# Attention logits with a 64-row second pass for two heads at once, and four steps put in another order

## Chip, cores and metric

One core of a Trainium2 chip runs the whole program. The metric is the device time of one execution in microseconds (us); less is better. Times of before: 2449.05, 2453.21 and 2453.59 us, median 2453.21.

## What is computed

Two sequences (512 and 256 tokens, width 1024) go through two layers in f32. They are held together as T = 768 tokens in six blocks of 128. A layer is:

```python
xn = rmsnorm(x, norm1_g[l]); z = xn @ w_in[l]
o_a = mixer_a(...)   # gelu, layer norm, a 128x128 mix inside each block
o_b = mixer_b(...)   # 8 query heads, 2 key heads, band of 3 blocks, bias and sink
o_c = mixer_c(...)   # 8 query heads, 2 key heads, all keys, q and k normed and rotated
merged = sum(sigmoid(xn @ w_gate + b_gate) * (o_n @ w_branch_n))
x = x + merged @ w_out[l]
x = x + conv_ffn(rmsnorm(x, norm2_g[l]), ...)   # up, conv of width 3, silu * val, down
```

A head has 64 channels, and its logits are q . k / 8, an inner product over 64.

## The kernel before

**Precision.** The large products are made of float32r passes, where an operand is its rounded part (hi) plus the rest (lo): w_hi x_hi + w_hi x_lo + w_lo x_hi, so three matmuls (L435, L564, L1121) for each product. ScalarE (ACT) writes each hi of a weight (L327, L337), VectorE (DVE) each lo (`Stream.flush`, L357). Weights arrive by DMA through SyncE (SP) into `raw` tiles and quarter tiles `qa` to `qd`; the FFN's up projection works with seven products P1 to P7 in place of eight (`piece`, L1110), for which GpSimd (POOL) adds quarters with accumulating DMAs (`sum1` to `sum4`, L275).

**Logits.** `attention` (L722) has 24 units in each of B and C per layer: a pair of heads (i) times a block of queries (n). `stage_a` (L742) makes the logits of head e of a unit, w = 256, 384 or 512 keys wide. A head's stationary operand has q_hi on 64 rows and q_lo on the other 64; the moving operand `kb[:, 0]` has k_hi on both halves, `kb[:, 1]` has k_lo on both. Two matmuls on 128 rows, one for each, add up to the logits of one head (L757). Then DVE adds the bias and takes the minimum (L766, L771), ACT takes the exponential (L768, L772), `stage_n` divides, `stage_b` transposes the probabilities (L796), and `stage_c` multiplies them with v (L809): there head 0 fills columns 0 to 63 of the array and head 1 columns 64 to 127. An order written out by hand sets the steps of a unit: `ORDER` = a of head 0, b0 of the unit before, n0, a1, c of two units before, b1, n1. Each step is a yield of a generator that the dense products pump between their own matmuls (`pump`, L400), so PE goes from a dense product to one attention step and back.

**Other places that the change touches.**
- `sumsq` (L494) squares one of eight x tiles on ACT and adds it to a sum. Tiles 2 to 5 are added by accumulating DMAs that POOL issues (L508), into two sums (even and odd tiles), the rest on DVE (L504, L506). `rstd_tok` (L510) sums over channels on PE (L514), POOL takes the power -1/2 (L520); `rstd_diag` and `rstd_bc` spread it over the partitions (L530 to L546). In layer 0 `rstd_tok` stands in the middle of the first dense product; in the FFN it stands after piece P5 of the first group, and `rstd_bc` after P1 of the second.
- The rotary tables of C: two tables g, each of two broadcast DMAs of 192 KB in packets of 256 bytes (L885), then DVE multiplies (L888). This is issued ahead of the key and value product of C (`dense_tok`, L958).
- The convolution of the FFN: `later(n, f)` (L422) runs a step after n ticks; a dense product ticks once per k (six matmuls), a piece twice. `CHAIN` gives the ticks of a group's steps (scale, centre tap on ACT, two outer taps on DVE, silu, product, hi, lo), `CHAIN_END` those of the last group, after which few down products are left. Both outer taps were one step, `taps` (L1061).
- `qknorm` (L891) writes q of C as [hi, lo] on the rows for both heads.

Of the kernel before, what the change touches and what calls it, by code (L numbers as in the profile page):

```python
# [18 lines left out]
P = 128  # L19
D = 1024  # L20
KD = D // P
# [9 lines left out]
D_FF = 2816  # L31
NJ = D_FF // P
FFC = [(0, 3), (3, 3), (6, 3), (9, 3), (12, 3), (15, 3), (18, 4)]
CHAIN = (2, 4, 6, 9, 11, 13, 15)
CHAIN_END = (1, 2, 3, 5, 6, 7, 8)
TAIL = 5
HT = T // 2
HW = T + 3
# [91 lines left out]
def encoder_kernel(ctx, tc, x_d, w_d, vec_d, ln_d, rope_d, gqk_d, oneh_d, relb_d, mask_d, id_d, y_d):  # L130
# [61 lines left out]
    def fl(ap):  # L192
        return ap.bitcast(F32)
# [215 lines left out]
    def finish_bg(n=0):  # L409
        while len(bg) > n:  # L410
            if next(bg[0][0], "end") == "end":
                bg.pop(0)
# [78 lines left out]
        if k is not None:  # L491
            sumsq(x_ap, k, new=lambda: unit(F32)[:, 0])

    def sumsq(x_ap, k, dve=False, new=None):  # L494

        n = x_ap.shape[-1]
        c = 0 if dve else k % 2
        sq = (new or page)()[:, 0:n]
        ACT.activation(sq, x_ap, AF.Square)
        if k == c:  # L500
            st["acc", c] = sq
            return
        if dve or k >= KD - 2:
            DVE.tensor_tensor(st["acc", 0], st["acc", 0], sq, ALU.add)  # L504
            if not dve and k == KD - 2:
                DVE.tensor_tensor(st["acc", 0], st["acc", 0], st.pop(("acc", 1)), ALU.add)  # L506
        else:
            POOL.dma_start(out=st["acc", c], in_=sq, accum_op=ALU.add)  # L508
# [69 lines left out]
    def layer_mixers(l, xs):  # L578
# [143 lines left out]
        def attention(qs, kbs, vtok, out, bias):  # L722
# [19 lines left out]
            def stage_a(u, e):  # L742
                i, si, b0, nb, n, lo, hi = units[u]
                w = (hi - lo) * P
                if e == 0:
                    if bias:
                        fetch(i)
                        fetch(i + 1)
                        nbt.pop(i - 1, None)
                    wt = 388 if bias else 512  # L750
                    S[u] = dict(lg=page(T + 8) if bias else [page(512), page(512)], nm=small(2), rs=small(4))
                s = S[u]
                ps = sps()
                kb = kbs[i // 2]
                q = qs[i][:, e, n * P:(n + 1) * P]
                for c in range(2):
                    PE.matmul(out=ps[:, 0:w], lhsT=q, rhs=kb[:, c, lo * P:hi * P], start=c == 0, stop=c == 1)  # L757
                mn = s["nm"][:, e:e + 1]
                su = s["rs"][:, e:e + 1]
                if bias:  # L760
                    lg = s["lg"][:, e * 388:e * 388 + w + 1]
                    h = 2 * i + e
                    j0 = (lo - n + 1) * P
                    sink = st["ns"][:, h:h + 1]
                    POOL.tensor_copy(lg[:, w:w + 1], sink)
                    DVE.tensor_tensor_reduce(lg[:, 0:w], ps[:, 0:w], nbt[i][:, e * 384 + j0:e * 384 + j0 + w],  # L766
                                             1.0, sink, ALU.add, ALU.min, accum_out=mn)
                    ACT.activation(lg, lg, AF.Exp, bias=mn, scale=-1.0, accum_out=su)  # L768
                else:
                    lg = s["lg"][e][:, 0:w]  # L770
                    DVE.tensor_tensor_reduce(lg, ps[:, 0:w], zero.broadcast_to([P, w]), 1.0, BIG, ALU.add, ALU.min, accum_out=mn)  # L771
                    ACT.activation(lg, lg, AF.Exp, bias=mn, scale=-1.0, accum_out=su)  # L772
# [109 lines left out]
        for g in range(2):  # L882
            gt = page()
            for s in range(2):
                POOL.dma_start(  # L885
                    out=gt[:, s * 384:(s + 1) * 384],
                    in_=bass.AP(gqk_d.tensor, gqk_d.offset + ((l * 2 + g) * 2 + s) * HD, [[0, P], [0, NT], [1, HD]]))
            DVE.scalar_tensor_tensor(gt, cs, -(HD ** -0.5) if g == 0 else 1.0, gt, ALU.mult, ALU.mult)  # L888
            tab.append(gt)

        def qknorm(z, nh, tb, cats, dst):  # L891
            n = nh * HD
            t1, t2 = (unit(F32).rearrange("p a b -> p (a b)")[:, 0:NT * n] for _ in range(2))

            def v4(u):
                return u.rearrange("p (t h d) -> p t h d", t=NT, d=HD)

            z4, t14, t24 = v4(z), v4(t1), v4(t2)
            ACT.activation(t2, z, AF.Square)
            yield  # L900
            cg = tb[:, 0:384].rearrange("p (t d) -> p t d", t=NT).unsqueeze(2)
            sg = tb[:, 384:768].rearrange("p (t d) -> p t d", t=NT).unsqueeze(2)
            DVE.tensor_tensor(t14, z4, cg.broadcast_to([P, NT, nh, HD]), ALU.mult)
            ss = small(24)[:, 0:NT * nh]
            DVE.tensor_reduce(ss, t2.rearrange("p (a d) -> p a d", d=HD), AX.X, ALU.add)
            DVE.tensor_scalar(ss, ss, 1.0 / HD, EPS, ALU.mult, ALU.add)
            rr = small(24)[:, 0:NT * nh]
            POOL.tensor_tensor(rr, ss, neghalf[:, 0:NT * nh], ALU.pow)
            yield
            for a in range(2):  # L910
                o, i = slice(a * 32, a * 32 + 32), slice(32 - a * 32, 64 - a * 32)
                DVE.tensor_tensor(t24[:, :, :, o], z4[:, :, :, i],
                                  sg[:, :, :, o].broadcast_to([P, NT, nh, 32]), ALU.mult)
            yield
            DVE.tensor_tensor(t1, t1, t2, ALU.add)
            yield
            t13 = t1.rearrange("p (a d) -> p a d", d=HD)
            DVE.tensor_tensor(t13, t13, rr.unsqueeze(2).broadcast_to([P, NT * nh, HD]), ALU.mult)
            yield
            us = []  # L920
            for i in range(2):
                u = unit()
                u4 = u.rearrange("p a b -> p (a b)").rearrange("p (t e x) -> p t e x", t=NT, e=2)
                if cats == "k":
                    for r in range(2):
                        ACT.activation(u4[:, :, 0, r * HD:(r + 1) * HD], t14[:, :, i], AF.Copy)
                else:
                    ACT.activation(u4[:, :, :, 0:HD], t14[:, :, 2 * i:2 * i + 2], AF.Copy)
                us.append(u4)
                yield  # L930
            for i, u4 in enumerate(us):
                if cats == "k":
                    for r in range(2):
                        DVE.tensor_tensor(u4[:, :, 1, r * HD:(r + 1) * HD], t14[:, :, i], fl(u4[:, :, 0, 0:HD]), ALU.subtract)
                else:
                    DVE.tensor_tensor(u4[:, :, :, HD:2 * HD], t14[:, :, 2 * i:2 * i + 2], fl(u4[:, :, :, 0:HD]), ALU.subtract)
                yield
            yield
            for u4 in us:
                u = unit()  # L940
                for e in range(2):
                    yield from tr6(lambda t: u4[:, t, e, :], identr,
                                   lambda ps, a, b: ACT.activation(u[:, e, a:b], ps, AF.Copy))
                dst.append(u)
# [12 lines left out]

        dense_tok(("in2", l, 1792 + 512, 0), ("in2", l, 1792 + 512, 1), xs, evac_kv)  # L958
        finish_bg()
        start_bg(qknorm(zk, 2, tab[1], "k", kc), BG_N)  # L960
        for c in range(2):
            z = flat(unit(F32))
# [75 lines left out]
    def layer_ffn(l, xs2, x_mid, x_spill):  # L1038
# [19 lines left out]
            ACT.activation(f, h[:, 1:770], AF.Identity, scale=cw(1, ct), bias=vec[:, VCB + ct:VCB + ct + 1])  # L1058
            return f

        def taps(f, h, ct):  # L1061
            DVE.scalar_tensor_tensor(f, h[:, 0:769], cw(0, ct), f, ALU.mult, ALU.add)
            DVE.scalar_tensor_tensor(f, h[:, 2:771], cw(2, ct), f, ALU.mult, ALU.add)

        def scaled(h):
            DVE.tensor_tensor(h[:, 1:770], h[:, 1:770], st["bcg"][:, 1:770], ALU.mult)  # L1066
# [1 line left out]
        def conv_v(g):  # L1068
            s = G[g]
            hv = s["h"][:, 1]  # L1070

            def c():
                s["fv"] = centre(hv, NJ + g)
            for n, f in zip(CHAIN_END if g == NJ - 1 else CHAIN,
                            (lambda: scaled(hv), c, lambda: taps(s["fv"], hv, NJ + g))):
                later(n, f)

        def conv_g(g):
# [23 lines left out]
                hs[g] = u  # L1102
                del G[g]
            for n, f in zip(CHAIN_END if g == NJ - 1 else CHAIN,
                            (lambda: scaled(hg), c, lambda: taps(s["fg"], hg, g), si, mu, hi, lo)):
                later(n, f)

        RIGHT = ((1 + HT, 513, 0, 512 - HT), (514, 770, 512 - HT, HT))
# [55 lines left out]
        def evac(c, m, cuts, ps):  # L1164
            last = c == len(FFC) - 1
            final_ = last and l == DEPTH - 1
            if final_:
                t0, t1 = cuts
                xa = st["xu"][m // 2][:, m % 2, t0:t1]
                DVE.tensor_tensor(xa, ps[:, 0, 0:t1 - t0], xa, ALU.add)  # L1170
                sumsq(xa, m, dve=True)
                if t0 and m == 2:
                    finish_bg()
                if m == KD - 1:
# [16 lines left out]
        for s in steps:  # L1191
            if s[0] == "pc":
                piece(s[1], s[2])
                if (s[1], s[2]) == (0, "P5"):
                    rstd_tok()
                    rstd_diag()
                elif (s[1], s[2]) == (1, "P1"):
# [56 lines left out]
    with tc.manual_schedule():  # L1254
# [17 lines left out]
        for k in range(KD):  # L1272
# [13 lines left out]
                W.split()  # L1286
                W.flush()
            if k > 2:
                sumsq(xu[(k - 3) // 2][:, (k - 3) % 2], k - 3)
        for k in range(KD - 3, KD):  # L1290
            sumsq(xu[k // 2][:, k % 2], k)
        del u, xu
        spill = [dram.tile([P, T], F32, name=f"sp{k}") for k in range(KD)]
        x_mid = [dram.tile([P, T], F32, name=f"xm{k}") for k in range(KD)]
# [135 lines left out]
```

## Time and profile before

| | |
|---|---|
| median of three runs | 2453.21 us |
| the profiled execution, its own time | 2457.03 us |
| its span, first to last instruction | 2455.3 us |
| mean granted TensorE clock | 0.989 of full |
| busy: PE / DVE / ACT / POOL | 97 / 62 / 45 / 11 % |
| moved by DMA | 328 MB |

PE is TensorE's matmul, PEld its weight load. In a row of a timeline the first number is the start, the second the duration of that row; a wait in brackets is the engine's idle time just before it and what ended it. In rows of groups the shape is rows*columns of the array, output <- input, then the count, and after the bar busy us and the mean ns of one. The parts of the kernel by time: start and mixer A to 120 us, mixers B and C to 552, projection out to 704, FFN to 1230; the second layer repeats it.

### The profile page before, as it was taken

The numbers are of one execution on the slowest core, as the hardware profiler recorded it, in microseconds if no ns is written. First come the engines' busy times: TensorE is split into PE (matmuls) and PEld (weight loads), VectorE is DVE, ScalarE is ACT, GpSimd is POOL, SyncE is SP. The second block draws the span as 40 slices with busy tenths as digits, with TensorE's granted clock in tenths as the row PEclk, the third lists the DMA queues.
The fourth block names the chain that finished last, engine by engine and source line by source line (L and its number), as shares of the span: only waits on it lengthen the run. The fifth ranks groups of instructions, "written<-read, shape, count | busy, mean of one in ns | idle before, by whom it ended". The sixth has DMA issues, their size and how long they took to land.

```text
span 2455.3 us, 38491 instructions
## 1 busy us (share of the span) xinstructions
PE 2388.1 (97%) x14990; PEld 2315.9 (94%) x14990; DVE 1523.8 (62%) x2656; ACT 1110.0 (45%) x2184; POOL 260.3 (11%) x390
## 2 busy tenths in 40 slices
PE   7999999999999999999999999999999999999997
PEld 7998999889989999999999999998899899999996
DVE  4555535554558777777645554555445687777785
ACT  4344434662345444444433443456424554444452
POOL 1000110000122111111000000100001211111100
PEclk8999999999999999999999999999999999999998
DMA  5511231012467888887732113210135688888854
GB/s 159 108 52 57 52 64 61 27 35 73 137 161 173 244 225 231 230 228 209 219 108 62 57 50 63 61 45 34 44 102 161 145 221 230 228 230 227 227 160 147
DMA packets 134950, 328.24 MB, mean 134 GB/s; under 512 B 15976, under 2 KB 29416, under 8 KB 134768
## 3 DMA queue, kind: packets, MB, share of 16 engines
q1 hardware_dynamic: 101232, 251.83, 31.6%
q0 software_dynamic: 33536, 73.95, 17.0%
q8 instruction: 118, 1.93, 0.3%
q14 instruction: 64, 0.52, 0.1%
HBM read 243.93 MB, written 52.43 MB: 121 GB/s over the span
## 4 chain that ended last, share of the span: by engine, by line
PE 85%; DMA 5%; DVE 4%; ACT 3%; issue 2%; POOL 0%; SPq 0%; POOLq 0%; DVEq 0%; ACTq 0%
PE d L435 47%; PE ga L1121 12%; PE gb L1121 9%; PE d L564 8%; PE s L809 3%; PE s L796 2%; PE s L757 2%; DMA qc<-w_pk 2%; DMA pg<-gqk 1%; DVE wl L357 1%; PE s L669 1%; ACT wh L327 1%; DMA qd<-qc 1%; DMA raw<-w_pk 1%; DMA pg<-pg 0%
## 5 line engine op out<-in xcount | busy, mean ns | idle before, releaser
L435 PE MATMUL d<-u,wh 128*128 128x384 f32 x4480 | 990.1, 343 | 6.8 <-ACT pg L1086 6.3
L435 PEld LDWEIGHTS d<-u,wh 128*128 128x128 f32 x4480 | 782.6, 189 | 21.8 <-issue 11.0
L435 PE MATMUL d<-u,wl 128*128 128x384 f32 x2240 | 575.3, 338 | 0.0
L435 PEld LDWEIGHTS d<-u,wl 128*128 128x128 f32 x2240 | 408.0, 188 | 0.0
L357 DVE TENSOR_TENSOR wl<-raw,wh 128x512 fp32r<-128x512 f32 (+1 forms) x261 | 248.4, 953 | 232.5 <-ACT wh L337 180.8
L1121 PE MATMUL ga<-u,wh 128*128 128x384 f32 x1408 | 364.5, 340 | 7.6 <-ACT u L1129 4.4
L1121 PE MATMUL gb<-u,wh 128*128 128x384 f32 x1056 | 271.0, 338 | 1.9 <-DVE u L1131 1.9
L1121 PEld LDWEIGHTS ga<-u,wh 128*128 128x128 f32 x1408 | 257.1, 189 | 9.5 <-ACT u L1129 5.0
L564 PE MATMUL d<-wh,u 128*128 128x256 f32 x1344 | 248.3, 285 | 3.0 <-ACT u L596 1.9
L1121 PE MATMUL ga<-u,wl 128*128 128x384 f32 x704 | 238.7, 339 | 0.0
L564 PEld LDWEIGHTS d<-wh,u 128*128 128x128 f32 x1344 | 210.9, 191 | 5.2 <-ACT u L596 3.1
L564 PE MATMUL d<-wl,u 128*128 128x256 f32 x672 | 190.7, 284 | 4.9 <-DVE wl L357 4.8
L1121 PEld LDWEIGHTS gb<-u,wh 128*128 128x128 f32 x1056 | 191.6, 188 | 2.7 <-ACT wh L327 1.8
L337 ACT ACTIVATE wh<-raw 128x1024 fp32r<-128x1024 f32 x129 | 135.3, 1049 | 104.3 <-PE d L564 44.9
L1121 PE MATMUL gb<-u,wl 128*128 128x384 f32 x528 | 178.0, 337 | 0.0
L1058 ACT ACTIVATE pg<-u,vec 128x769 f32<-128x769 f32 x88 | 91.0, 1034 | 124.5 <-DVE u L1066 82.0
L1180 DVE TENSOR_TENSOR pg<-d,pg 128x768 f32<-128x768 f32 x104 | 99.5, 956 | 76.5 <-PE d L435 76.0
L564 PEld LDWEIGHTS d<-wl,u 128*128 128x128 f32 x672 | 128.6, 191 | 5.5 <-DVE wl L357 5.2
L1121 PEld LDWEIGHTS ga<-u,wl 128*128 128x128 f32 x704 | 133.2, 189 | 0.0
L662 DVE TENSOR_TENSOR u<-s,u 128x128 fp32r<-128x128 f32 (+1 forms) x112 | 36.9, 329 | 114.5 <-ACT u L661 114.3
L757 PE MATMUL s<-u,u 128*128 128x256 f32 (+2 forms) x384 | 99.9, 342 | 2.2 <-ACT pg L797 1.6
L768 ACT ACTIVATE pg<-pg,sm 128x257 f32<-128x257 f32 (+1 forms) x96 | 52.5, 547 | 109.1 <-DVE sm L766 104.7
(204 smaller groups left out, 3190.1 us busy)
## 6 DMA issues: line engine op xcount, KB each, us to landing
raw<-w_pk SPq DMA_DIRECT2D x174, 512.0 KB, 3.7
pg<-xm SPq DMA_DIRECT2D x104, 384.0 KB, 4.6
xm<-pg SPq DMA_DIRECT2D x96, 384.0 KB, 3.4
u<-w_pk SPq DMA_DIRECT2D x96, 192.0 KB, 3.6
qa<-w_pk SPq DMA_DIRECT2D x44, 256.0 KB, 3.8
qb<-w_pk SPq DMA_DIRECT2D x44, 256.0 KB, 3.2
qc<-w_pk SPq DMA_DIRECT2D x44, 256.0 KB, 3.2
qd<-w_pk SPq DMA_DIRECT2D x44, 256.0 KB, 3.5
```

The costliest lines, as they stand in the source:

```text
L337: ACT.activation(hi[:, :n], t[:, :n], AF.Copy)
L357: DVE.tensor_tensor(lo, t, fl(hi), ALU.subtract)
L435: PE.matmul(out=ps[:, h, 0:b - a], lhsT=w, rhs=x[:, a:b], start=first and i == 0 and pi == 0, stop=last and i == nk - 1 and pi == 2,)
L564: PE.matmul(out=outs[t], lhsT=x, rhs=w, start=k == 0 and pi == 0 and t % 2 == 0, stop=k == KD - 1 and pi == 2, skip_group_check=True)
L662: DVE.tensor_tensor(u[:, 1, a:b], ps, fl(u[:, 0, a:b]), ALU.subtract)
L757: PE.matmul(out=ps[:, 0:w], lhsT=q, rhs=kb[:, c, lo * P:hi * P], start=c == 0, stop=c == 1)
L768: ACT.activation(lg, lg, AF.Exp, bias=mn, scale=-1.0, accum_out=su)
L796: PE.transpose(ps[:, b * P:(b + 1) * P], lg[:, b * P:(b + 1) * P], ident)
L809: PE.matmul(out=ps[e * HD:(e + 1) * HD, 0:P], lhsT=vtok[:, (lo + b) * P + kv * HD:(lo + b) * P + (kv + 1) * HD], rhs=pT, start=b == 0, sto ...
L1058: ACT.activation(f, h[:, 1:770], AF.Identity, scale=cw(1, ct), bias=vec[:, VCB + ct:VCB + ct + 1])
L1121: PE.matmul(out=o, lhsT=a[:, w], rhs=x[:, b], start=p in ("P1", "P2", "P5") and kp == 0 and pi == 0, stop=kp == 3 and pi == 2, skip_group_ ...
L1180: DVE.tensor_tensor(h2(xa), ps[:, :, 0:384], h2(xa), ALU.add)
```

## The change

Head 1's logits are made in head 0's step. Of each head's two matmuls the second keeps only the rows of q_hi (64), so that head 0's is on rows 0 to 63 and head 1's on rows 64 to 127; the order is (head 0, 128 rows), (head 0, 64), (head 1, 64), (head 1, 128). C's q is laid out for it as B's was: q_hi of head 1 on the upper rows. In the start, the squares are added one after another by DVE and POOL instructions. `rstd_tok` of the FFN comes after P6, one piece sooner. The tables are multiplied after the key and value product. The two outer taps are two steps, with new ticks.

```diff
-CHAIN = (2, 4, 6, 9, 11, 13, 15)
-CHAIN_END = (1, 2, 3, 5, 6, 7, 8)
+CHAIN = (2, 4, 6, 7, 9, 11, 13, 15)
+CHAIN_END = (1, 2, 4, 5, 6, 8, 9, 10)
...
-    def sumsq(x_ap, k, dve=False, new=None):
+    def sumsq(x_ap, k, eng=None, new=None):
-        c = 0 if dve else k % 2
+        c = 0 if eng else k % 2
...
-        if dve or k >= KD - 2:
-            DVE.tensor_tensor(st["acc", 0], st["acc", 0], sq, ALU.add)
-            if not dve and k == KD - 2:
+        if eng or k >= KD - 2:
+            (eng or DVE).tensor_tensor(st["acc", 0], st["acc", 0], sq, ALU.add)
+            if not eng and k == KD - 2:
...
-                ps = sps()
-                kb = kbs[i // 2]
-                q = qs[i][:, e, n * P:(n + 1) * P]
-                for c in range(2):
-                    PE.matmul(out=ps[:, 0:w], lhsT=q, rhs=kb[:, c, lo * P:hi * P], start=c == 0, stop=c == 1)
+                if e == 0:
+                    kb = kbs[i // 2]
+                    s["ps"] = [sps(), sps()]
+                    for a, c in ((0, 0), (0, 1), (1, 1), (1, 0)):
+                        r = slice(a * HD, a * HD + HD) if c else slice(0, P)
+                        PE.matmul(out=s["ps"][a][:, 0:w], lhsT=qs[i][r, a, n * P:(n + 1) * P], rhs=kb[r, c, lo * P:hi * P],
+                                  start=a == c, stop=a != c)
+                ps = s["ps"][e]
...
-            DVE.scalar_tensor_tensor(gt, cs, -(HD ** -0.5) if g == 0 else 1.0, gt, ALU.mult, ALU.mult)
             tab.append(gt)
...
-                    ACT.activation(u4[:, :, :, 0:HD], t14[:, :, 2 * i:2 * i + 2], AF.Copy)
+                    for e in range(2):
+                        ACT.activation(u4[:, :, e, e * HD:(e + 1) * HD], t14[:, :, 2 * i + e], AF.Copy)
...
         finish_bg()
+        for g in (1, 0):
+            DVE.scalar_tensor_tensor(tab[g], cs, -(HD ** -0.5) if g == 0 else 1.0, tab[g], ALU.mult, ALU.mult)
         start_bg(qknorm(zk, 2, tab[1], "k", kc), BG_N)
...
-                            (lambda: scaled(hg), c, lambda: taps(s["fg"], hg, g), si, mu, hi, lo)):
+                            (lambda: scaled(hg), c, lambda: tap(s["fg"], hg, g, 0), lambda: tap(s["fg"], hg, g, 2), si, mu, hi, lo)):
...
-                if (s[1], s[2]) == (0, "P5"):
+                if (s[1], s[2]) == (0, "P6"):
                     rstd_tok()
                     rstd_diag()
...
-                sumsq(xu[(k - 3) // 2][:, (k - 3) % 2], k - 3)
+                sumsq(xu[(k - 3) // 2][:, (k - 3) % 2], k - 3, DVE if k % 2 == 0 else POOL)
         for k in range(KD - 3, KD):
-            sumsq(xu[k // 2][:, k % 2], k)
+            sumsq(xu[k // 2][:, k % 2], k, DVE)
```

The lo of C's q (L936) and the steps of `conv_v` change likewise.

## Rows read from the trace of the kernel before

**Rows 1.** Waits of PE: who waited for whom, total us, times, longest us

```profile
PE s L514 <- DVE pg L504: 9.5, 1, 9.5
PE d L435 <- ACT pg L1086: 6.3, 2, 3.2
PE d L564 <- DVE wl L357: 4.8, 2, 3.2
...
PE d L544 <- ACT pg L531: 3.8, 2, 2.9
```

**Rows 2.** Stretches (length, busy us of PE, PEld, DVE, ACT, POOL, granted clock, DMA)

```profile
25.80:39.50 13.70, 7.54 (x35) 7.55 (x36) 6.76 (x10) 2.69 (x6) 4.10 (x7) 0.50 0.67 159
326.20:329.60 3.40, 3.25 (x15) 3.25 (x16) 1.23 (x2) 0.00 (x0) 0.00 (x0) 0.50 0.56 176
722.10:729.00 6.90, 5.86 (x17) 5.26 (x18) 3.38 (x6) 4.05 (x9) 0.84 (x1) 0.51 0.69 122
1189.80:1193.20 3.40, 3.40 (x12) 3.40 (x12) 3.30 (x6) 1.46 (x3) 0.00 (x0) 0.50 0.92 309
```

**Rows 3.** Groups of instructions, shapes kept apart: the logits' matmuls

```profile
L757 PE MATMUL s<-u,u 128*128 128x512 f32 x128 | 42.4, 415 | 1.5 <-ACT pg L797 0.9 <-ACT sd L797 0.6
L757 PE MATMUL s<-u,u 128*128 128x256 f32 x192 | 40.5, 292 | 0.7 <-ACT pg L797 0.7
...
L757 PE MATMUL s<-u,u 128*128 128x384 f32 x64 | 17.0, 346 | 0.0
```

**Rows 4.** The chain that ended last: a stretch of dense matmuls, 384 columns each

```profile
552.22 151.43 PE d L435 x864
```

**Rows 5.** Timeline of PE through one `stage_c`, between 128-column matmuls (384 wide, then transposes)

```profile
442.09 0.52 PE L435 MATMUL d<-u,wl 128*128 128x384 f32 x2
442.53 0.32 PE L809 MATMUL s<-sd,pg 128*64 128x128 f32 x1
442.54 0.32 PE L809 MATMUL s<-pg,pg 128*64 128x128 f32 x1
442.69 0.27 PE L809 MATMUL s<-sd,pg 128*64 128x128 f32 x1
...
443.35 0.27 PE L809 MATMUL s<-sd,pg 128*64 128x128 f32 x1
...
443.56 0.66 PE L796 MATMUL s<-ident,pg 128*128 128x128 f32 x4
```

**Rows 6.** Timeline of PE: first two dense matmuls after a 32*8 one (L468)

```profile
60.41 0.39 PE L564 MATMUL d<-wh,u 128*128 128x256 f32 x1
60.63 0.28 PE L564 MATMUL d<-wl,u 128*128 128x256 f32 x1
```

**Rows 7.** Timeline of DVE in the start

```profile
18.19 1.02 DVE L490 SCALAR_TENSOR_TENSOR u<-u,vec,u 128x768 fp32r<-128x768 f32 x1 [0.54 <-ACT u L489]
27.11 0.96 DVE L504 TENSOR_TENSOR pg<-pg,pg 128x768 f32<-128x768 f32 x1 [7.91 <-DMA pg<-pg]
...
30.94 0.96 DVE L504 TENSOR_TENSOR pg<-pg,pg 128x768 f32<-128x768 f32 x1
```

**Rows 8.** The chain that ended last: the rotary tables' DMAs in layer 0

```profile
305.23 18.89 DMA pg<-gqk
```

**Rows 9.** Timeline of POOL: the norm of the FFN in layer 0

```profile
713.80 0.86 POOL L275 DMA_DIRECT2D qc<-w_pk  x1 [7.24 <-DMA qc<-w_pk]
...
718.80 0.84 POOL L275 DMA_DIRECT2D qd<-qc  x1 [3.28 <-DMA qc<-w_pk]
719.37 1.66 POOL L520 TENSOR_TENSOR sm<-sm,neghalf 128x6 f32<-128x6 f32 x1
```

**Rows 10.** Timeline of DVE: the last group's chain in layer 0

```profile
1182.24 1.01 DVE L1062 SCALAR_TENSOR_TENSOR pg<-u,vec,pg 128x769 f32<-128x769 f32 x1
...
1185.10 1.02 DVE L1101 TENSOR_TENSOR u<-pg,u 128x512 fp32r<-128x512 f32 x2
...
1188.28 0.95 DVE L1180 TENSOR_TENSOR pg<-d,pg 128x768 f32<-128x768 f32 x1
```

More of the change, by code (lines that the diff above doesn't have):

```diff
@@ L935, in qknorm @@
                 else:
-                    DVE.tensor_tensor(u4[:, :, :, HD:2 * HD], t14[:, :, 2 * i:2 * i + 2], fl(u4[:, :, :, 0:HD]), ALU.subtract)
+                    for e in range(2):
+                        DVE.tensor_tensor(u4[:, :, e, (1 - e) * HD:(2 - e) * HD], t14[:, :, 2 * i + e],
+                                          fl(u4[:, :, e, e * HD:(e + 1) * HD]), ALU.subtract)
                 yield
@@ L1059, in centre, with tap @@
             return f
-        def taps(f, h, ct):
-            DVE.scalar_tensor_tensor(f, h[:, 0:769], cw(0, ct), f, ALU.mult, ALU.add)
-            DVE.scalar_tensor_tensor(f, h[:, 2:771], cw(2, ct), f, ALU.mult, ALU.add)
+        def tap(f, h, ct, k):
+            DVE.scalar_tensor_tensor(f, h[:, k:769 + k], cw(k, ct), f, ALU.mult, ALU.add)
         def scaled(h):
@@ L1074, in conv_v @@
             for n, f in zip(CHAIN_END if g == NJ - 1 else CHAIN,
-                            (lambda: scaled(hv), c, lambda: taps(s["fv"], hv, NJ + g))):
+                            (lambda: scaled(hv), c, lambda: tap(s["fv"], hv, NJ + g, 0), lambda: tap(s["fv"], hv, NJ + g, 2))):
                 later(n, f)
@@ L1170, in evac @@
                 DVE.tensor_tensor(xa, ps[:, 0, 0:t1 - t0], xa, ALU.add)
-                sumsq(xa, m, dve=True)
+                sumsq(xa, m, DVE)
                 if t0 and m == 2:
```

## The prediction, made before the change was run

> **What bounds the kernel now.** I began with the page's busy shares, as the table above gives them: PE is busy in 97% of the span, DVE in 62%, ACT in 45%. Whatever adds or takes PE time inside a stage that keeps PE full therefore counts in full, and work of DVE, ACT or POOL counts only where PE stands behind it. Next the waits of PE [rows 1], of which the reader should see four that belong to edits of the change: 9.5 us before the norm's sum in the start, 6.3 us in two waits near the FFN's end, 4.8 us in two at the lo of a weight beside the rotary tables, 3.8 us in two before the spread of the FFN's norm. The first of the two FFN-end waits names ACT's silu, but what PE needs there is a free accumulator, as shown below. [...] Last, at the level of single instructions, the logits and what PE does when it changes the part of the array it uses [rows 3 to 6].
>
> **The start.** Today two accumulating DMAs in each of two sums hold up the first add on DVE by 7.91 us, and the last add ends at 30.94 + 0.96 = 31.9 us [rows 7]. After the change the order on DVE is: add of tile 3, lo of x tile 7, then adds 5 to 7, with tiles 2 and 4 added by POOL in between. No row shows POOL adding 768 elements. The nearest are DVE's add of this shape, 0.96 us [rows 7], and POOL's power on only 6 elements, 1.66 us [rows 9]; a slow POOL is bounded by the chain ending no sooner than it does now. I take 2.0 us, twice DVE's, since POOL's fixed part looks large. The add of tile 3 then ends near 18.8 us, which pushes the lo of tile 7 from 18.19 to 18.8 [rows 7]; PE waits for this lo, but the 0.6 us only eat into its later wait. POOL adds tile 4 until 20.8, three adds of 0.96 follow, and the sum is ready at 23.7 in place of 31.9: 8.2 us. Each us more on POOL's add costs 2, so at 6.1 us nothing is left, and at 0.96 it is 10.3. Of the 13.7 us at half clock 7.54 were busy [rows 2], so 3.8 us were lost; a wait of about 1 us may still cost some of it, so I take 3.0. Start: 11.2 us less (0 to 13.3).
>
> [...]
>
> **The tables.** Their last DMA takes 18.89 us and lands at 324.1 [rows 8]. DVE waits for it with two splits of weights queued behind, and PE waits for those: 4.8 us in two waits, the longest 3.2 [rows 1], and 1.6 us in layer 0 by the clock (3.25 busy at 0.50 [rows 2]). Moved behind the product, the same wait stands at its end. Next in DVE's queue are then the key norm, which is paced and early, and a split that PE needs only a half product later, 72 matmuls of 256 columns, over 8 us; two multiplications and one split take about 3. Cover enough: 6.4 us less (bounds 4 and 6.4). If the DMA landed 5 us later, the wait would be back.
>
> **The norm of the FFN.** POOL's power stands behind an accumulating DMA of the next group (718.80), whose issue waits 3.28 us for the one issued at 713.80 [rows 9]. One piece earlier in the program, the power is queued directly behind the issue at 713.80, which is done at 714.7. PE's sum, 12 matmuls of 0.175 or 2.1 us sooner than now, is ready about then, so POOL runs the power some 4.5 us sooner than at 719.37, more than the longest wait of 2.9 [rows 1]. The accumulating DMAs it passes go out later by at most its 1.66 us, and the one at 718.80 was waiting anyway; SP's loads are not passed. That frees 3.8 us of waits in both layers [rows 1] and half of 5.86 us at half clock [rows 2], 6.7 in all. But the quarters' chain (load, accumulate, accumulate) follows close: the second half of rows 9 is its DMAs waiting on each other. I keep 5.0 (2 to 6.7).
>
> **The last group.** DVE runs both taps of the value (from 1182.24), the scale, a lo (1185.10) and, after a wait for ACT's centre tap, both taps of the gate before the accumulator of the first down product is emptied at 1188.28, done 1189.2 [rows 10]. PE's third product needs that accumulator and has then waited 3.2 us [rows 1], since 1186.0. So this wait is DVE's queue. With the new ticks only one scale, the two value taps and the lo stand ahead: 1182.24 plus three times about 1.0, the lo's 1.02 and its own 0.95 [rows 10] is about 1187.2, a wait near 1.1, and with so short a wait I expect no half clock (1.7 us today [rows 2]). The gate's taps come after, and silu to lo end two ticks later, still before the last down products read them. Per layer 2.1 + 1.7 = 3.8 (L435's other wait of 3.2 is the same place in layer 1); both layers 7.6 less (4 to 9.7).
>
> Costed at nothing: the split tap in all other groups (same DVE work) and q's copies in two halves (eight more instructions on each of DVE and ACT, well under an add's 0.96 us [rows 7] apiece). DVE and ACT are idle for over a third of the span, and no wait in rows 1 is at these copies. If that cover were gone it would be at most 8 us.
>
> **The logits.** What goes: one pass per unit, if the two 64-row passes run beside each other. A dense matmul of 384 columns takes 151.43 / 864 = 175 ns [rows 4], so by columns 233, 175 and 117 ns for 512, 384 and 256. The counts [rows 3], four to a unit, make 32, 16 and 48 units: 32 x 233 + 16 x 175 + 48 x 117 = 15.9 us.
>
> Does it run side by side? For columns it does: head 0's and head 1's matmuls on half the columns start 0.01 us apart (442.53, 442.54) [rows 5], and the pairs follow at (443.35 - 442.69) / 6 = 0.11 us. Their output banks are separate here, and so I take it for rows too.
>
> What comes: entering and leaving a split array. Going in: 442.09 to 442.53 is 0.44 for two matmuls of 0.175, so 0.09 extra; the next pair comes after 0.16 in place of 0.11, 0.05 more [rows 5], the weight load that could not be hidden, 64 columns. Going out: 443.35 (pair) to 443.56 is 0.21 in place of 0.11, 0.10 extra [rows 5]; and the second matmul after it starts 60.63 - 60.41 = 0.22 later in place of 0.117, another 0.103 [rows 6], the unhidden load of 128 columns. No row shows a switch by rows alone. Its bounds are no cost at all, if the rows need no switch, and these four terms with the load of 128 columns on both sides: 0.09 + 0.103 + 0.10 + 0.103 = 0.40 us a visit. I take the upper end, since both kinds of smaller tile in the trace paid it at both edges, one of them 32 rows high. 96 units x 0.40 = 38.4 us, so the logits lose 38.4 - 15.9 = 22.5 us (-15.9 to +22.5; if the passes don't run side by side, +38.4).
>
> [...]
>
> Head 1's logits now lie ready while DVE and ACT still work on head 0; some of the short waits of PE in B and C should go, 1 us less (0 to 4). Against it, head 1's bank of the four is held two steps longer; DVE empties it two steps before it is asked for.
>
> **Sum.** -11.2 - 6.4 - 5.0 - 7.6 + 22.5 - 1.0 = -8.7 us against the profiled execution's 2457.03, which is 3.8 above the median; on the median, 2453.2 - 8.7 = 2444.5 us. So four repairs of 30.2 us are mostly paid back by the logits.
>
> **Rivals.**
> *The rows need no switch* (chance 0.25). For: the passes of one pair use the same rows and columns that the 128-row matmul before them uses. Against: rows 5 and 6. The logits win 15.9: 2453.2 - 30.2 - 15.9 - 1 = 2406 us.
> *The switch is paid and the two passes still run one after the other* (0.12): slower. Place: L757 between its second and third matmul; price 15.9 us more, so 38.4 on the logits, 2453.2 - 30.2 + 38.4 - 1 = 2460.4 us. It decides as soon as the logits cost over 31 us. For: no row shows two row halves at work together; against: the column pairs [rows 5].
> *The pass isn't made smaller, but nothing is switched either* (0.07): 64 rows take as long as 128 and the array stays as it is, the change doing nothing for the logits: 2453.2 - 31 = 2422 us.
>
> **Numbers.** My forecast has 0.56. Within 0.2% (4.9 us) a measurement of this kernel can't tell it from no change. All bounds of its repairs one way would give 2436 and 2466; as they are independent, its own range is 2436 to 2459, and in it I give 0.62 to faster, 0.28 to same, 0.10 to slower. With the rivals: faster 0.35 + 0.25 + 0.07 = 0.67, same 0.16 + 0.02 = 0.18, slower 0.05 + 0.10 = 0.15. The range must take in most of the no-switch case, so 2402 to 2459; above it lies most of the serial case, and a little on both sides.
>
> **What would show it.** Right: PE starts the norm's sum near 24 us; no wait of PE at L357's lo beside the tables; POOL's power ahead of the accumulating DMA; the waits at the FFN's end near 1 us; head 0's and head 1's 64-row matmuls 0.01 us apart, with 0.09 us extra ahead and 0.2 behind them, and mixers B and C of each layer some 11 us longer. Wrong: logits matmuls following each other at 117 to 233 ns without a gap (first rival), the third one a full pass after the second (second rival), or POOL's adds over 4 us.

## The result, and the profile after

The changed kernel takes **2472.05 us** (median of five runs, 2464.48 to 2474.6) against 2453.21: ratio 1.0062, 95% interval 1.0048 to 1.0077, slower by 0.6%. Run again in a later comparison it was 1.0075 (1.0060 to 1.0090). The forecast was 2444.5 us with 2459 as the upper end: wrong in sign, by 27.5 us. The profiled execution is the fastest one, 2464.48 us with a span of 2462.7, only 7.4 us over the span of before. The profile of the second comparison has 2474.7; its stretches at half clock (0.50 granted) add up to 55.0 us within the span against 38.7 here, and half of the difference, 8.2 us, is most of the 12 between the two.

Lines have moved: the logits are L758 (L757 before), DVE's reading of them L769 and L774 (L766, L771), the last group's accumulator L1186 (L1180), the tables' multiplication L966 (L888).

The waits of PE in the changed kernel (who waited for whom, total us, times, longest us):

```profile
PE d L564 <- issue: 4.2, 1, 4.2
PE s L758 <- DVE sm L774: 3.8, 3, 1.3
...
PE d L435 <- ACT u L657: 2.7, 1, 2.7
PE s L758 <- DVE sm L769: 2.3, 1, 2.3
...
PE d L435 <- DVE pg L1186: 1.9, 2, 0.9
...
PE s L669 <- ACT u L928: 1.7, 1, 1.7
PE d L564 <- ACT u L971: 1.6, 1, 1.6
```

The four that the change aimed at [rows 1] have gone or shrunk: no L514 in the start, 0.9 instead of 3.2 at the last down product, none before the spread of the FFN's norm, none behind L357's lo. All other rows here are new or larger than before (L435 on L657 had 0.5).

**The logits came as forecast.** Timeline of PE through one visit of 256 columns, answering to [rows 5]:

```profile
445.48 0.34 PE L435 MATMUL d<-u,wl 128*128 128x384 f32 x1
445.65 0.28 PE L758 MATMUL s<-u,u 128*128 128x256 f32 x1
445.86 0.39 PE L758 MATMUL s<-u,u 64*128 64x256 f32 x2
446.18 0.38 PE L758 MATMUL s<-u,u 128*128 128x256 f32 x1
446.40 0.34 PE L435 MATMUL d<-u,wh 128*128 128x384 f32 x1
```

A dense pass of 256 columns is 0.117, two thirds of the 0.175 for 384 [rows 4]. The two 64-row passes start 0.003 us apart, and from there to the start of the fourth matmul it is 0.315 us at 256 columns and 0.428 at 512 (medians): 256 columns more cost one pass more, not two, so they run side by side. Going in costs 445.86 - 445.65 - 0.117 = 0.09, going out 446.18 - 445.86 - 0.117 = 0.20, and the pass after that 0.22 - 0.117 = 0.10. Together 0.39 a visit, for a pass saved of 0.117. The same landmarks on all 96 units give 0.386 on average: 37.1 - 15.9 = 21.2 us (forecast 22.5).

**The start.** Timelines of POOL, then DVE, answering to [rows 7]:

```profile
15.76 2.37 POOL L504 TENSOR_TENSOR pg<-pg,pg 128x768 f32<-128x768 f32 x1 [13.73 <-ACT pg L499]
19.96 2.48 POOL L504 TENSOR_TENSOR pg<-pg,pg 128x768 f32<-128x768 f32 x1 [1.83 <-DVE pg L504]
```

```profile
22.47 3.08 DVE L504 TENSOR_TENSOR pg<-pg,pg 128x768 f32<-128x768 f32 x3 [1.72 <-POOL pg L504]
```

POOL's add takes 2.4 us (I took 2.0), and the sum is ready at 25.5 instead of 31.9.

**The FFN's norm** went as its step said. POOL, answering to [rows 9]:

```profile
721.70 0.86 POOL L275 DMA_DIRECT2D qc<-w_pk  x1 [7.21 <-DMA qc<-w_pk]
722.29 1.65 POOL L520 TENSOR_TENSOR sm<-sm,neghalf 128x6 f32<-128x6 f32 x1
723.63 1.19 POOL L275 DMA_DIRECT2D raw<-qd  x1
```

The power is now directly behind the issue that it used to come long after.

**The tables went the other way.** The chain that ended last, in layer 0, and below it DVE's timeline:

```profile
308.94 23.69 DMA raw<-w_pk
...
332.89 0.95 DVE pg L966
333.84 1.14 DVE wl L357
```

```profile
332.01 1.83 DVE L966 SCALAR_TENSOR_TENSOR pg<-pg,pg 128x768 f32<-128x768 f32 x2 [14.32 <-DMA pg<-gqk]
```

At its new place DVE still waits 14.3 us for the same DMAs, until 332.0, which is 7.9 us later than they landed before (324.1 [rows 8]), and beside them a weight load takes 23.69 us. Stretches at 0.50 of the clock follow the new waits on L657, on L769 and on "issue" (columns as in [rows 2]):

```profile
89.30:92.70 3.40, 3.40 (x12) 3.40 (x12) 2.39 (x5) 1.06 (x1) 0.00 (x0) 0.50 0.67 122
181.50:184.90 3.40, 3.40 (x13) 3.30 (x12) 2.37 (x10) 1.08 (x5) 0.00 (x0) 0.50 0.29 119
1540.00:1543.40 3.40, 3.40 (x18) 3.40 (x17) 3.29 (x5) 1.79 (x2) 0.00 (x0) 0.50 0.04 11
```

### The profile page after: what moved, and what is told of

Read it like the earlier page. It is cut to its first block, busy times and chain, and to the rows that moved or that the text cites. A ratio compares the mean times of both kernels' runs of the same rounds, so it can differ in the third digit from the quotient of the medians.

```text
span 2462.7 us, 38520 instructions
## 1 busy us (share of the span) xinstructions
PE 2408.9 (98%) x14990; PEld 2301.3 (93%) x14990; DVE 1525.4 (62%) x2666; ACT 1114.5 (45%) x2192; POOL 261.0 (11%) x388
## 4 chain that ended last, share of the span: by engine, by line
PE 85%; DMA 4%; DVE 4%; issue 3%; ACT 3%; POOL 0%; SPq 0%; POOLq 0%; DVEq 0%; ACTq 0%
PE d L435 48%; PE ga L1127 12%; PE gb L1127 9%; PE d L564 7%; PE s L758 3%; PE s L812 3%; PE s L799 2%; DMA raw<-w_pk 2%; DMA qb<-w_pk 1%; DVE wl L357 1%; DMA qc<-w_pk 1%; PE s L669 1%; ACT wh L337 0%; ACT wh L327 0%; PE s L639 0%
## 5 line engine op out<-in xcount | busy, mean ns | idle before, releaser
L435 PE MATMUL d<-u,wh 128*128 128x384 f32 x4480 | 993.6, 343 | 4.7 <-ACT u L657 2.7
L435 PEld LDWEIGHTS d<-u,wh 128*128 128x128 f32 x4480 | 783.0, 189 | 17.9 <-issue 13.4
L435 PE MATMUL d<-u,wl 128*128 128x384 f32 x2240 | 575.8, 338 | 0.0
L435 PEld LDWEIGHTS d<-u,wl 128*128 128x128 f32 x2240 | 408.3, 188 | 0.0
L357 DVE TENSOR_TENSOR wl<-raw,wh 128x512 fp32r<-128x512 f32 (+1 forms) x261 | 248.3, 952 | 225.6 <-ACT wh L337 188.6
L1069 DVE SCALAR_TENSOR_TENSOR pg<-u,vec,pg 128x769 f32<-128x769 f32 x176 | 179.0, 1017 | 2.1
L1186 DVE TENSOR_TENSOR pg<-d,pg 128x768 f32<-128x768 f32 x104 | 99.4, 956 | 70.7 <-PE d L435 70.2
L758 PE MATMUL s<-u,u 64*128 64x256 f32 (+5 forms) x384 | 106.4, 412 | 7.2 <-DVE sm L774 3.8
```

The lines of the kernel that those rows point to most:

```text
L357: DVE.tensor_tensor(lo, t, fl(hi), ALU.subtract)
L435: PE.matmul(out=ps[:, h, 0:b - a], lhsT=w, rhs=x[:, a:b], start=first and i == 0 and pi == 0, stop=last and i == nk - 1 and pi == 2,)
L758: PE.matmul(out=s["ps"][a][:, 0:w], lhsT=qs[i][r, a, n * P:(n + 1) * P], rhs=kb[r, c, lo * P:hi * P], start=a == c, stop=a != c)
L1069: DVE.scalar_tensor_tensor(f, h[:, k:769 + k], cw(k, ct), f, ALU.mult, ALU.add)
L1186: DVE.tensor_tensor(h2(xa), ps[:, :, 0:384], h2(xa), ALU.add)
```

## The experiments

The table adds up where each profile differs from that of before. The n-th dense matmul is the same one in every kernel, so the difference of its start in two traces is what was won or lost up to there (us; less is faster; both layers together).

| run | start, to 101 | mixer B | tables and C | FFN norm | FFN end, rest | span |
|---|---|---|---|---|---|---|
| changed | -6.0 | 11.8 | 19.1 | -10.7 | -6.7 | +7.4 |
| changed, again | -2.4 | 13.0 | 21.6 | -5.8 | -6.9 | +19.4 |
| logits back | -5.3 | 0.8 | 8.0 | -7.1 | -6.9 | -10.4 |
| logits only | 2.5 | 12.4 | 18.2 | -0.7 | -1.5 | +31.0 |
| start, norm, tail | -5.9 | 0.8 | 3.1 | -9.4 | -6.9 | -18.3 |
| narrow tables | -3.4 | -0.7 | -7.1 | -6.9 | -6.9 | -25.0 |
| together, full | -2.4 | 2.8 | 15.4 | -1.7 | -6.6 | +7.5 |
| dead packets | -5.8 | 0.7 | 10.4 | -2.6 | -7.1 | -4.4 |
| tab in parts | -8.8 | -0.7 | -8.5 | -7.0 | -7.1 | -32.0 |

Single profiles scatter by 2 to 4 us in a column, even where nothing was changed (first and norm columns of "logits only"), so sums are taken from the medians of the timed runs. Runs 1, 2, 5 and 6 were timed in one comparison, runs 3, 4, 7 and 9 in a second, both of 8 in a third. The median of before moved between them (2460.22, 2455.83 and 2454.44 us), so kernels are compared by their ratios; by their intervals, a difference of two ratios is uncertain by some 0.2%, 5 us.

**1. The logits of before in the changed kernel** (C's q stays laid out as changed).

```diff
-                if e == 0:
-                    s["ps"] = [sps(), sps()]
...
+                ps = sps()
+                for c in range(2):
+                    PE.matmul(out=ps[:, 0:w], lhsT=q, rhs=kb[:, c, lo * P:hi * P], start=c == 0, stop=c == 1)
```

> The changed kernel with the logits of before: each head's two matmuls on 128 rows, in its own step; everything else as changed. Theory (the switch to two row halves is the price): the trace of the changed kernel gives 0.386 us for each of 96 visits, 37.1 us, less 15.9 us for the pass saved, so this run is 21 us faster than the changed kernel, 2451 us (2446 to 2456). Rival 1 (issuing both heads in one step costs as well, by waits for the banks of head 1): some 8 us more, about 2443. Rival 2 (the logits are a small part, and what was lost was lost at the rotary tables or elsewhere): above 2460.

Measured: 2445.68 us, 0.9949 of before (0.9932 to 0.9965), so 1.0075 - 0.9949 = 1.26% or 31 us faster than the changed kernel (28 us by the first comparison's 1.0062). The logits are the larger part of the loss, and cost more than the switch's 21 us: rival 1.

**2. The logits alone, on the kernel before** (with C's q layout).

```diff
-                for c in range(2):
-                    PE.matmul(out=ps[:, 0:w], lhsT=q, rhs=kb[:, c, lo * P:hi * P], start=c == 0, stop=c == 1)
+                if e == 0:
+                    s["ps"] = [sps(), sps()]
...
```

> The kernel before with the logits of the change alone (and the layout of C's q that they need). Theory: 21 us slower than before, 2474 us (2470 to 2480). Rival 1 (the waits for head 1's banks come with it): about 29 us slower, 2482. Rival 2 (logits a small part): under 2463.

Measured: 2483.63, 1.0103 (1.0087 to 1.0119): 25 us slower, between theory and rival 1. Mixer B alone, where no table is near, pays 12.4 us.

**3. Both heads together, but on 128 rows.** This takes the 31 us apart.

```diff
-                        r = slice(a * HD, a * HD + HD) if c else slice(0, P)
-                        PE.matmul(out=s["ps"][a][:, 0:w], lhsT=qs[i][r, a, n * P:(n + 1) * P], rhs=kb[r, c, lo * P:hi * P],
+                        PE.matmul(out=s["ps"][a][:, 0:w], lhsT=qs[i][:, a, n * P:(n + 1) * P], rhs=kb[:, c, lo * P:hi * P],
```

> The changed kernel, with both heads' logits still made in head 0's step, but all four matmuls on 128 rows: the banks are held as in the change, and no row half is used. Theory (two terms: 0.386 us for each switched visit, 37.1 - 15.9 = 21.2 us in all, and some 8 us of new waits, because head 1's bank is taken two steps sooner): 8 us slower than the run with the logits back, 0.3% of it. Rival 1 (issuing together is free): as fast as that run. Rival 2 (the row halves cost nothing, issuing together is the whole loss): 23 us slower than it, as slow as the changed kernel.

Measured: 2452.62, 0.9983 (0.9972 to 0.9994). Against run 1 that is 0.34%, 8.4 us (3.5 to 13 by the intervals): the price of issuing the heads together. Against the changed kernel beside it, 1.0075 - 0.9983 = 0.92% or 22.6 us: the price of the row halves, as the forecast had it; in the two traces, from the first matmul of each unit to the one behind its fourth, it is 22.6 us over all units once the waits are taken off. Behind the 8.4 stand 7.2 us of waits that neither run 1 nor before has:

```profile
PE s L757 <- DVE sm L773: 4.8, 4, 1.5
...
PE s L757 <- DVE sm L768: 2.4, 1, 2.4
```

How one arises, in the changed kernel: PE, then DVE:

```profile
1665.13 0.92 PE L758 MATMUL s<-u,u 128*128 128x512 f32 x2
1667.33 0.92 PE L758 MATMUL s<-u,u 64*128 64x512 f32 x2 [1.27 <-DVE sm L774]
```

```profile
1664.84 1.23 DVE L357 TENSOR_TENSOR wl<-raw,wh 128x1024 fp32r<-128x1024 f32 x1 [1.95 <-ACT wh L337]
1665.99 0.15 DVE L783 RECIPROCAL sm<-sm 128x1 f32<-128x1 f32 x1
1666.18 0.49 DVE L787 TENSOR_SCALAR pg<-pg,sm 128x512 f32<-128x512 f32 x1
1666.58 0.68 DVE L774 CUSTOM_DVE_ANT_0 pg<-s,zero 128x512 f32<-128x512 f32 x1
```

Head 1's pair needs one of four banks, and that bank still holds logits that DVE reads at 1666.58, because a lo of weights (1.23 us) and two steps of the softmax stand ahead. Where head 1 asks for its bank two steps later, as in run 1 and before, no such wait is there.

**4. The row halves apart**, so that the array is switched twice a unit.

```diff
-                    for a, c in ((0, 0), (0, 1), (1, 1), (1, 0)):
+                    for a, c in ((0, 0), (0, 1), (1, 0), (1, 1)):
```

> The changed kernel, with the order (head 0, 128 rows), (head 0, 64), (head 1, 128), (head 1, 64): two visits of a row half for each unit instead of one, and the halves no longer side by side. Theory: one more visit of 0.386 us for each of 96 units is 37 us, and the 15.9 us that ran side by side come back: 53 us slower than the changed kernel. Rival 1 (the extra time comes only where two halves run at once): 16 us slower. Rival 2 (the going in and out is hidden when a single half is used, one weight load at a time): about the same as the changed kernel.

Measured: 2518.02, 1.0255 (1.0239 to 1.0271): 1.8% or 44 us slower than the changed kernel beside it, nearer to the theory's 53 than to 16. PE's timeline:

```profile
459.56 1.22 PE L758 MATMUL s<-u,u 128*128 128x256 f32 x4
460.71 0.44 PE L435 MATMUL d<-u,wh 128*128 128x384 f32 x1
```

The visit takes 460.71 - 459.56 = 1.15 us in place of 0.75, and the second dense matmul behind it starts 0.28 us after the first in place of 0.18. So the second visit costs 0.40 + 0.10 - 0.117 = 0.39 us besides its pass; over all units this trace is 47 us longer up to there, or 0.33 a visit once the passes' 15.9 are taken off. A single row half pays nearly as much as a pair: the price hangs on the change of shape, not on two halves at work.

**5. Start, norm and tail alone**: run 1 with the tables back at their old place and C's q laid out as before (not shown in the diff).

```diff
+            DVE.scalar_tensor_tensor(gt, cs, -(HD ** -0.5) if g == 0 else 1.0, gt, ALU.mult, ALU.mult)
             tab.append(gt)
...
-        for g in (1, 0):
-            DVE.scalar_tensor_tensor(tab[g], cs, -(HD ** -0.5) if g == 0 else 1.0, tab[g], ALU.mult, ALU.mult)
```

> The kernel before with the start's sum, the FFN's norm and the last group's chain of the change; logits and tables as before. By the changed kernel's trace the three are worth 10.6 + 10.4 + 6.7 = 27.7 us, so 2425 us (2420 to 2432). Theory on the tables (their move gives nothing, as the weight loads that it sets free run into the broadcast's small packets): this run is as fast as the run with the logits back, within 4 us. Rival (the move gains its 6.4 us): this run is 6 us slower than that one. Rival (the move loses): faster than that one by over 5 us.

Measured: 2438.79, 0.9919 (0.9905 to 0.9933), 21 us faster than before, and 6.9 us faster than run 1 beside it (2 to 12 by the intervals). Between the dense matmuls at 303 and 345 us of before, and between those at 1510 and 1560, run 1 loses 1.9 and 4.4 us against run 5; q's copies, the other thing that differs, run only at 367 and 1563 us. So the move of the tables loses, and the third case holds. DMA issues from 296 to 336 us (KB each, median us from issue to landing) in run 5, then in run 1:

```profile
raw<-w_pk SPq DMA_DIRECT2D x3, 512.0 KB, 3.7
```

```profile
raw<-w_pk SPq DMA_DIRECT2D x3, 512.0 KB, 17.8
```

In run 5 the first of these weight loads is issued 2.2 us after the tables' last DMA has landed, in run 1 2.9 us after it was issued; there the load takes 25.3 us, and that DMA 27.4 us in place of 19.7. The missing 6 of the 27.7 us are in the first column of the table: what the start wins by 45 us it gives back in part at 86 (run 8).

**6. Narrow tables**: run 5, with each broadcast bringing its 64 columns once; VectorE repeats them.

```diff
-                    out=gt[:, s * 384:(s + 1) * 384],
-                    in_=bass.AP(gqk_d.tensor, gqk_d.offset + ((l * 2 + g) * 2 + s) * HD, [[0, P], [0, NT], [1, HD]]))
+                    out=gt[:, s * HD:(s + 1) * HD],
+                    in_=bass.AP(gqk_d.tensor, gqk_d.offset + ((l * 2 + g) * 2 + s) * HD, [[0, P], [1, HD]]))
...
+                                         gt[:, s * HD:(s + 1) * HD].unsqueeze(1).broadcast_to([P, NT, HD]), ALU.mult, ALU.mult)
```

> As the run with start, norm and tail alone, but each of the four broadcast DMAs of the rotary tables brings 64 columns once in place of six times (32 KB in place of 192 KB), and VectorE repeats them by its access pattern in the multiplication, which stays where it was before. Theory (the wait at the tables is the time that many packets of 256 bytes need): a sixth of the packets land before VectorE asks for them, the 4.8 us of waits and 1.6 us at half clock go: 6.4 us faster than the run with start, norm and tail alone, 2419 us. Rival (the DMAs land late because they are issued late behind other work, whatever their packets): no faster than that run.

Measured: 2429.63, 0.9884 (0.9870 to 0.9897): 9.2 us faster than run 5 (the repeat in run 8 gives less), and no wait of PE at the tables is left.

**7. Dead packets**: run 6, and in addition the four full broadcasts into pages that nothing reads.

```diff
+        for g in range(2):
+            dead = page()
+            for s in range(2):
+                POOL.dma_start(
+                    out=dead[:, s * 384:(s + 1) * 384],
+                    in_=bass.AP(gqk_d.tensor, gqk_d.offset + ((l * 2 + g) * 2 + s) * HD, [[0, P], [0, NT], [1, HD]]))
```

> As the run with the narrow tables, and in addition the four full broadcasts of 192 KB in packets of 256 bytes into two pages that nothing reads (a dead load). No engine waits for them. Theory (the packets themselves hold up what shares their DMA engines: weight loads and the fetches of PE's instructions): PE stands again near the key and value product of C, 3 to 5 us in a layer with nothing that the trace names or behind the weights' lo, and 6 to 12 us of the 9 are lost again. Rival (only the engine that waits for the tables loses): within 2 us of the narrow tables.

Measured: 2448.87, 0.9973 (0.9964 to 0.9983). 0.89% or 22 us are lost to transfers that no engine waits for (0.60% or 15 us against the repeat of run 6 in run 8), more than the 6 to 12 I expected; 17.5 of them stand in the table's column of tables and C (10.4 + 7.1). DMA issues from 296 to 336 us again, in before, changed, narrow tables and dead packets:

```profile
raw<-w_pk SPq DMA_DIRECT2D x4, 512.0 KB, 3.5
pg<-gqk POOLq DMA_DIRECT2D x4, 192.0 KB, 16.7
pg<-rope POOLq DMA_DIRECT2D x2, 192.0 KB, 2.6
```

```profile
raw<-w_pk SPq DMA_DIRECT2D x4, 512.0 KB, 9.9
pg<-gqk POOLq DMA_DIRECT2D x4, 192.0 KB, 20.3
```

```profile
raw<-w_pk SPq DMA_DIRECT2D x4, 512.0 KB, 3.6
...
pg<-gqk POOLq DMA_DIRECT2D x4, 32.0 KB, 3.1
```

```profile
raw<-w_pk SPq DMA_DIRECT2D x3, 512.0 KB, 20.6
pg<-gqk POOLq DMA_DIRECT2D x4, 192.0 KB, 20.5
```

The same 192 KB take 2.6 us for `rope` and 16.7 for `gqk`, and the four weight loads issued beside `gqk` in the changed kernel took 16.1 to 24.1 us, one in run 7 26.4. In before, DVE's wait for the tables had the weights' lo queued behind it, so SP's next load wasn't issued until they had landed, and took 3.5 us. The moved multiplication frees the load to start inside the broadcast. The chain of the dead packets shows what waits for it:

```profile
304.73 26.43 DMA raw<-w_pk
331.18 1.07 ACT wh L337
332.27 1.23 DVE wl L357
...
338.09 0.97 DVE u L930
```

The key norm, which I had called paced and early, stands behind that split on DVE, and PE waits 6.3 us for it.

**8. The bias table in parts**: run 6, where mixer B's table (2 MB in one DMA) is made in four, two of them later; and **run 6 again** beside it.

```diff
-        td = dram.tile([8, P, 512], F32, name="tab")
-        POOL.dma_start(out=td, in_=tb[0:8, :].unsqueeze(1).broadcast_to([8, P, 512]))
+        st["tb"] = dram.tile([8, 512], F32, name="tb")
+        POOL.dma_start(out=st["tb"], in_=tb[0:8, :])
...
+            POOL.dma_start(out=td, in_=st["tb"][2 * j:2 * j + 2, :].unsqueeze(1).broadcast_to([2, P, 512]))
```

> As the run with the narrow tables, and the bias table of mixer B (2 MB in one DMA, 44 us) is made in four parts from a small copy, two of them at the old place and the other two when they are next to be needed. Theory (the start gives back 2 to 4 us at about 90 us, because the weight load that now comes due there runs beside this one DMA): the wait of 2.3 us at L435 on ACT's L657 and the stretch at half clock behind it go, 4 us faster than the narrow tables on the same chip, 0.16%. Rival (that load is late for its own place in SyncE's queue): no faster, the wait stays above 2 us.

> The narrow tables again, beside the run with the bias table in parts. As before: 1.2% faster than the kernel before (0.9884); a ratio over 0.991 would say that the first one was luck of its chip.

Measured: 2423.99, 0.9875 (0.9862 to 0.9889), and the narrow tables beside it 2433.62, 0.9913 (0.9898 to 0.9927), just over the line I had set, so part of the first 0.9884 counts as luck. The two ratios stand for about 1% together, so against run 5 the narrow tables gain between 1.5 and 9 us; in the repeat's trace the column of tables and C is -7.1 as in the first. In parts it is 0.38% or 9 us faster than that, more than the 4 expected; in the table the first column wins 5.4 us on "narrow tables", and the wait at L657 is gone. DMA issues from 50 to 100 us, in the changed kernel and in this one:

```profile
raw<-w_pk SPq DMA_DIRECT2D x5, 512.0 KB, 14.0
tab<-pg POOLq DMA_DIRECT2D x1, 2048.0 KB, 44.1
```

```profile
raw<-w_pk SPq DMA_DIRECT2D x6, 512.0 KB, 4.0
tab<-tb POOLq DMA_DIRECT2D x3, 512.0 KB, 15.2
```

This is the version that beats both kernels: 1.25% under before.

**9. The changed kernel again**, no edit.

> The changed kernel again, beside the others. If the parts add up (start, norm and tail -21.4, moved tables +6.9, logits +23.4, each as its run gave it) it is 9 us slower than before, 0.36%. Rival (they meet each other, as the first comparison of 0.62% says): 15 us slower; then this trace shows a wait that none of the single parts has.

Measured: 2474.65, 1.0075 (1.0060 to 1.0090), 18.4 us slower. The parts as I had them add up to 9. With run 1's 31 us for the logits the sum would come out, but that proves nothing, since the 31 are this kernel less run 1. Run 2 is independent: 25 us by its ratio, and -21.4 + 6.9 + 25 = 11, where the interval here is 15 to 22. No wait is in this trace that the single parts lack. Whether the logits cost more here (28 to 31 us) than on the kernel before (25) stays open; the intervals overlap.

## Why the prediction was wrong

Term by term, forecast and measured (start, norm and tail as the means of the table's rows that have them, without the bias table in parts; tables from the medians of runs 5 and 1, logits from the ratios of runs 9, 3 and 1; these three are uncertain by some 5 us each):

| step | forecast | measured |
|---|---|---|
| start | -11.2 | -4.5 |
| tables | -6.4 | +6.9 |
| FFN norm | -5.0 | -6.3 |
| last group | -7.6 | -6.9 |
| logits, switch and pass | +22.5 | +22.6 |
| logits, waits | -1.0 | +8.4 |
| sum | -8.7 | +20.2 |

Measured as a whole: +18.8 and +18.4.

- **Right:** the switch. The sum of its four costs, taken from the column tiles in [rows 5, 6], held for rows (0.39 against 0.40 us a visit), and the halves ran side by side. The loads that the prediction calls not hidden show in PEld's rows of before: behind the first matmul of a new shape the next load starts 0.06 us after it at 64 columns (442.59 after 442.53) and 0.11 at 128 (60.52 after 60.41), later loads 0.01 after theirs (442.70 after 442.69, 60.64 after 60.63). The rivals fall: the two without a switch by run 3, the serial case by the 0.003 us between the two starts.
- **Right:** the last group, -3.4 us in each layer (3.8 forecast), with a wait of 0.9 (1.1) and no stretch at 0.50 behind it; and the norm, though between single profiles it varies from -1.7 to -10.7.
- **Wrong, the tables:** "Cover enough: 6.4 us less (bounds 4 and 6.4)". The cover was counted in DVE's and PE's work alone. The step left out what the wait had kept apart: SP's loads behind the lo's that were queued behind it. I wrote that a DMA landing 5 us later would bring the wait back, but gave it no chance and no cause; it came 7.9 us later in layer 0, and the change itself was the cause: it let a weight load start beside the broadcast, which took 23.7 us (25.3 in run 1) in place of 3.4 and held up the splits and the key norm behind it (runs 1, 5 and 7). Worth 13.3 us.
- **Wrong, the waits of the logits:** "DVE empties it two steps before it is asked for". The steps are in order, but DVE's queue also holds the dense product's lo's (1.23 us each). Worth 9.4 us.
- **Too large, the start:** the chain ends 6.4 us sooner rather than 8.2, as POOL's add takes 2.4 us and other work on DVE holds the add of tile 3 until 18.87. By 45 us the gain is 9.8 us in this trace and 6.1 in the repeat, where PE still waits 1.6 us at L514 and the half clock lasts 6.8 us in place of 3.4. Of either, 3.8 are lost again at 86: a load that took 20.9 us beside the bias table takes 23.2, ACT has it in its queue ahead of L657, and PE waits 2.7 us there and then runs at half clock. Worth 6.7 us.

The tables and the waits alone turn -8.7 into +14. The range's bounds for them allowed no loss, where the row said only that something waits there now.

## What to carry to other kernels

A wait in one queue can be what keeps two transfers apart (here a weight load of 3.4 us became one of 23.7): before moving it, list the DMAs that its queue holds back, and what else is on the DMA engines at that time. Using part of the array's rows pays only if the visit saves more than the way in and out, here 0.39 us, or three passes of 256 columns. A bank that is asked for earlier is asked of the whole queue of the engine that empties it, other work included (here 1.27 us of wait, with a lo of 1.23 us ahead).

## What was not expected of the hardware

**PE stops with no operand missing.** The 4.2 us of "issue" in the changed kernel, like the 5.2 us in run 1, is a stop in the middle of a product for which the profile shows no operand missing. PE's timeline in run 1, and the DMA queues there (packets, MB, share of 16 engines), two rows for 288.5 to 325 us, where q8 has none, and one for 325 to 326:

```profile
327.37 0.59 PE L564 MATMUL d<-wh,u 128*128 128x256 f32 x2 [5.21 <-issue]
```

```profile
q0 software_dynamic: 375, 1.16, 47.5%
q1 hardware_dynamic: 345, 1.26, 11.4%
...
q8 instruction: 1, 0.02, 6.0%
```

The instruction queue's packet comes at 325.0, after none for 36 us, and PE goes on 2.3 us later. With narrow tables the same stretch has two:

```profile
q8 instruction: 2, 0.03, 0.3%
```

In all five profiles with such a stop (the changed kernel twice, runs 1, 3 and 4) PE goes on 2.2 to 2.4 us after the packet begins, and the stop begins inside the broadcast. In these five the packet comes 36 to 38 us after the one before it; beside the tables' broadcasts that didn't stop PE, no more than 32. That PE waits for what this packet brings, and the packet for the broadcast, is read from this coincidence, and run 7 has the broadcast without such a stop; a kernel that delays the packet alone wasn't tried.

**The broadcast cost far more than its bytes**: 16.7 us against 2.6 for 192 KB, in pieces of 256 bytes rather than 1536. Part of the 16.7 is overlap: the four `gqk` DMAs are in flight at the same time. From the first issue to the last landing, before's four take 21.4 us for 768 KB and the two of `rope` 3.2 us for 384 KB, 3.4 times as long for each byte. The pieces of 256 bytes, which I called packets, are those of the access pattern; the profile counts larger packets (375 for 1.16 MB in the rows above). Whether the size of the pieces does it, or that all of them read the same few bytes, no run told apart.
